# Split rows at byte 128 of 512, and one matmul of zeros in six gate blocks

## The chip, the cores and the metric

The kernel runs on one core of one Trainium2 chip. The metric is the device time of one execution in microseconds; the time of a kernel is the median of its runs. The engines are TensorE (PE, with its weight loads PEld), VectorE (DVE), ScalarE (ACT), GpSimd (POOL) and SyncE (SP), which issues the transfers of the weights.

## The reference

Two transformer blocks run one after the other on 256 tokens of width 1024, in float32. The first has two attentions, a gate and a feed-forward part; the second a gated delta rule with a sparse latent attention, a cross attention on 256 tokens of memory, and a feed-forward part of the same size. Cut to the parts that this text is about:

```python
# first block, D_FF = 2816
h = h + rms_norm(merged @ w_out, post_mix_gain)
u = rms_norm(h, pre_ffn_gain)
gate_up = u @ w_ffn_in                                   # 1024 -> 2 x 2816
f = (silu(gate_up[..., :D_FF]) * gate_up[..., D_FF:]) @ w_ffn_out
h = h + rms_norm(f, post_ffn_gain)
...
# second block
x = x + jnp.concatenate([o_dn, o_dsa], axis=-1) @ w_out
hx = rmsnorm(x, g_xattn)
qx = (hx @ w_xq).reshape(b, s, X_HEADS, X_DH)            # keys, values: mem @ w_xkv
...
x = x + ox @ w_xo
hf = rmsnorm(x, g_ffn)
x = x + (jax.nn.silu(hf @ w_gate) * (hf @ w_up)) @ w_down
return rmsnorm(x, g_final)
```

## The kernel before

Activations lie feature by feature: a tile of 1024 features by 256 tokens is 128 partitions by eight rows of 256 float32 numbers, 1024 bytes a row. A matmul on PE holds a 128 x 128 block of weights and streams one such row through it: the moving row.

A product is made of three matmuls in the format `float32r`: each operand is split into a high part (rounded) and a low part (the rest). For the weights `load_w` does it: a transfer on SP brings 512 KB into `raw`, ACT casts it to `wh` (L311), DVE subtracts to `wl` (L313); each has three buffers. For activations `split` does the same (`uh`, `ul`, and likewise `od`, `m`, `mem`, `mix`, `ox`, `f` with `_h` and `_l`). `gemm` makes one block of 128 output features: 24 matmuls, all at L326. Over the eight k they alternate `uh` x `wh` and `ul` x `wh`, sixteen in all, and then come eight of `uh` x `wl`; they add up in one bank of PSUM. A block is 24 matmuls whatever its activations are called.

`ffn_in` is a feed-forward stage's first half: for 22 values of j it makes a gate block (columns 2j of `w_gu`) and an up block (2j + 1), 44 blocks; DVE, ACT and POOL multiply, apply silu and split the result into `f_h`, `f_l`. `post_norm` ahead of the first stage and `residual` ahead of the second make `us`, the eight pairs of rows (uh, ul) that it reads, and return the norm's factors. `post_norm` and `residual` also run the blocks of `w_out1`, `w_fo1`, `w_out2` and `w_xo`; `gemm_long` is `gemm` over more than eight k. The blocks of `w_xq` (cross attention) read `us` of the same kind. `mem_keys` multiplies the memory's `mem_h`, `mem_l`, and it stands ahead of the first feed-forward stage.

Where a row starts in its partition follows from the tile's start and its row length. `new_u` makes tiles of [128, 8, 272] numbers of which 256 a row are used, so the rows lie 1088 bytes apart, which is 64 more than a multiple of 512. The first `u` of all is made in another way, as one long row of numbers from which eight rows of 256 are taken at number AT = 112:

```python
uh, ul = (gpool.tile([P, KT * NT + P], F32R, name="u" + e, tag="u" + e)[:, AT:AT + KT * NT].rearrange(
    "p (a b) -> p a b", a=KT) for e in "hl")
```

`sumsq` squares on ACT (`sq`, L403) and adds on DVE (L404). The order of each engine's instructions is chosen by a scheduler when the program is built, from the order of the code; a few lines are pinned. Tiles are placed, and buffers of a tag are added where memory is free, by the same step.

Of the kernel before, what the change touches and what calls it, by code (L numbers as in the profile page):

```python
# [16 lines left out]
F32 = mybir.dt.float32  # L17
F32R = mybir.dt.float32r
# [7 lines left out]
P = 128  # L26
NT = 256
NM = 16
NK = NT + NM
NP = NT + 32  # L30
D = 1024
KT = D // P
FF = 2816
FT = FF // P
# [175 lines left out]
GATES = [int(c) for c in "0010202020302022"]  # L210
BDLAST = 0
WARM = 12
AT = 112
RB = 2
MAGIC = float(0x5F3759DF)
SWAP = [i ^ 16 for i in range(32)]
# [4 lines left out]
def _program(tc, d, out):  # L221
    nc = tc.nc
    ctx = ExitStack()
    pe, act, dve, pool, sp = nc.tensor, nc.scalar, nc.vector, nc.gpsimd, nc.sync
# [7 lines left out]
    with ctx:  # L232
# [4 lines left out]
        gpool = new_pool(ctx, "gen")  # L237
# [75 lines left out]
            eng.tensor_tensor(l[:, :kt * c], raw[:, :kt * c], h[:, :kt * c].bitcast(F32), OP.subtract)  # L313
            return h, l

        def gemm(src, xs, n, use, first=True, last=True, ps=None, raw=None, late=()):

            kt = len(xs)
            h, l = load_w(src, kt, raw=raw)
            if ps is None:  # L320
                ps = mm.tile([P, 512], F32, name="mm", tag="mm")
            o = ps[:, :n]
            soon = [k for k in range(kt) if k not in late]
            steps = [(w, k, i) for ks in (soon, late) for w, i2 in ((h, 2), (l, 1)) for k in ks for i in range(i2)]
            for n_, (w, k, i) in enumerate(steps):
                pe.matmul(o, w[:, k * P:(k + 1) * P], xs[k][i], start=(first and n_ == 0),  # L326
                          stop=(last and n_ == len(steps) - 1))
            if last and use is not None:
                use(o)
            return ps  # L330
# [78 lines left out]
        def new_u():  # L409
            uh = gpool.tile([P, KT, NK], F32R, name="uh", tag="uh")  # L410
            ul = gpool.tile([P, KT, NK], F32R, name="ul", tag="ul")
            return uh, ul

# [5 lines left out]
        apool = new_pool(apx, "a")  # L422

        u = gpool.tile([P, KT, NK], F32, name="u", tag="u")
        uh, ul = (gpool.tile([P, KT * NT + P], F32R, name="u" + e, tag="u" + e)[:, AT:AT + KT * NT].rearrange(
            "p (a b) -> p a b", a=KT) for e in "hl")

        st = opool.tile([P, 512], F32, name="st", tag="o")
# [4 lines left out]
        for k in range(1, KT, 2):  # L433
            n = min(2, KT - k)
# [55 lines left out]
        at = ExitStack()  # L490
# [14 lines left out]
        def bank():  # L505

            began[0] += 1
            return ppool.tile([P, 512], F32, name="s", tag="s") if began[0] <= 3 else None
# [331 lines left out]
        rsm = mhp.tile([P, NT], F32, name="rsm")  # L840
        act.activation(rsm, st[:, :NT], AF.Copy)

        def post_norm(src_w, xs, gain, res, res_out, g_next, whole=False):

            fg = mpool.tile([P, 8, NT], F32, name="fg", tag="fg")
            acc = gpool.tile([P, NK], F32, name="acc", tag="acc", bufs=1)[:, :NT]
            for j in range(8):
                def use(o, j=j):
                    act.activation(fg[:, j, :], o, AF.Copy, scale=G(gain, j))
                    sumsq(j, o, acc, NT)  # L850
                gemm_long(src_w[j], xs, NT, use)
            rr = gpool.tile([P, NK], F32, name="rs", tag="rs", bufs=2)
            rsqrt_of(opool, acc, ones_d, NT, rr[:, :NT])
            if whole:
                u = gpool.tile([P, KT, NK], F32, name="u", tag="uh")
            else:
                uh, ul = new_u()
            acc2 = gpool.tile([P, NK], F32, name="acc2", tag="acc2", bufs=1)[:, :NT]
            for j in range(8):
                dve.tensor_tensor(fg[:, j, :], fg[:, j, :], rr[:, :NT], OP.mult)  # L860
                pool.tensor_tensor(res_out[:, j, :], fg[:, j, :], res[:, j, :NT], OP.add)
                if whole:
                    act.activation(u[:, j, :NT], res_out[:, j, :], AF.Copy, scale=G(g_next, j))
                else:
                    split(uh[:, j, :NT], ul[:, j, :NT], res_out[:, j, :], G(g_next, j))
                sumsq(j, res_out[:, j, :], acc2, NT)
            rs2 = gpool.tile([P, NK], F32, name="rs", tag="rs", bufs=2)
            rsqrt_of(opool, acc2, ones_d, NT, rs2[:, :NT])
            if whole:
                return [u[:, k, :NT] for k in range(8)], rs2[:, :NT]  # L870
            return [(uh[:, k, :NT], ul[:, k, :NT]) for k in range(8)], rs2[:, :NT]

        h1 = rpool.tile([P, KT, NT], F32, name="h1", tag="resB")
        us, rs = post_norm(d["w_out1"], [(m_h[:, k, :], m_l[:, k, :]) for k in range(8)],
                           "post_mix", hT, h1, "pre_ffn")

        def ffn_in(pool_, src_w, us, rs, f_h, f_l):
            for j in range(FT):
                sg = pool_.tile([P, NT], F32, name="sg", tag="sg", bufs=3)

                def use_g(o, sg=sg):
                    dve.tensor_tensor(sg, o, rs, OP.mult)  # L882
                    act.activation(sg, sg, AF.Silu)  # L883
                    pool.tensor_tensor(sg, sg, rs, OP.mult)  # L884

                def use_u(o, sg=sg, j=j):
                    t = pool_.tile([P, NT], F32, name="ft", tag="ft", bufs=2)
                    dve.tensor_tensor(t, o, sg, OP.mult)  # L888
                    split(f_h[:, j, :], f_l[:, j, :], t)

                bank = lambda i: ppool.tile([P, 512], F32, name="s", tag="s") if 2 * j + i < 3 else None
                gemm(src_w[2 * j], us, NT, use_g, ps=bank(0))
                gemm(src_w[2 * j + 1], us, NT, use_u, ps=bank(1))
            tc.keep_in_program_order(act.preload_act_table_set(EXP_LN))

# [64 lines left out]
        triu = CB("triu")  # L960
        ones_q = carve(P)
        dve.memset(ones_q, 1.0 / 256)
        mix_h = bpool.tile([P, 8, NT], F32R, name="mix_h")
        mix_l = bpool.tile([P, 8, NT], F32R, name="mix_l")

        sa = ExitStack()
        spool = new_pool(sa, "sa")
# [556 lines left out]

        added = []

        def residual(src_w, xs, res, res_out, g_next, late=(), more=0):
            uh, ul = new_u()
            acc = gpool.tile([P, NK], F32, name="acc", tag="acc", bufs=1)[:, :NT]
            for j in range(8):  # L1530
                def use(o, j=j):
# [7 lines left out]
            return [(uh[:, k, :NT], ul[:, k, :NT]) for k in range(8)], rs2[:, :NT]  # L1539

        x2 = rpool.tile([P, KT, NT], F32, name="x2", tag="resB")
        us, rs = residual(d["w_out2"], [(mix_h[:, k, :], mix_l[:, k, :]) for k in range(8)], x1, x2, "g_xattn", (0,1,2,3), 2)
        b2.close()


# [10 lines left out]
            return h, l  # L1556
        keys = [two("kx_", kx[:, 2 * h:2 * h + 2, :]) for h in range(4)]
        values = [two("vx_", vx[:, :, h * NT:(h + 1) * NT]) for h in range(4)]
        ox_h = xpool.tile([P, 8, NT], F32R, name="ox_h")
        ox_l = xpool.tile([P, 8, NT], F32R, name="ox_l")  # L1560
        rx = xpool.tile([P, 4], F32, name="rx")

        def query_scale():
# [41 lines left out]
                    pe.matmul(o[:, e, :], v_h, pt_l[:, mk, :], start=False, stop=(mk == 1))  # L1605
            split(ox_h[:, 2 * h:2 * h + 2, :], ox_l[:, 2 * h:2 * h + 2, :], o)
        x3 = rpool.tile([P, KT, NK], F32, name="x3", tag="resA")[:, :, :NT]
        us, rs = residual(d["w_xo"], [(ox_h[:, k, :], ox_l[:, k, :]) for k in range(8)], x2, x3, "g_ffn", (4,5,6,7), 2)
        xa.close()
        mst.close()  # L1610

# [7 lines left out]
        for qb in range(2):  # L1619
            for kk_ in range(2):  # L1620
# [1 line left out]
                for i in range(4):  # L1622
                    pe.transpose(t[:, i * P:(i + 1) * P], x3[:, 4 * kk_ + i, qb * P:(qb + 1) * P], ident)
                dve.tensor_copy(x3t[:, qb, kk_ * 512:(kk_ + 1) * 512], t)
        f_h = mpool.tile([P, FT, NT], F32R, name="f_h")
        f_l = mpool.tile([P, FT, NT], F32R, name="f_l")
        ffn_in(mpool, d["w_gu2"], us, rs, f_h, f_l)
        b1.close()
        accp = new_pool(fst, "ps_acc", 1, PSUM)
# [75 lines left out]
```

## Time and profile before

| | |
|---|---|
| time, median of 3 runs | 1013.58 us (1012.79 to 1014.91) |
| the profiled execution, its own time | 1014.82 us |
| its span | 1013.0 us |
| granted clock of PE, mean | 0.986 |
| busy: PE, PEld | 983.6 us (97%), 911.2 us (90%) |
| busy: DVE, ACT, POOL | 686.3 us (68%), 530.1 us (52%), 236.0 us (23%) |
| read from memory | 147.01 MB, 146 GB/s over the span |

Busy time counts an engine as busy while any of its instructions runs; matmuls overlap in the pipeline, so a busy PE says nothing of how closely they follow each other. That is read from the starts of matmuls in the timeline.

### The profile page before, as it was taken

To read this page: it belongs to the slowest core of one execution; us is meant where nothing else is said; L and a number is where in the kernel's file an instruction comes from. 1 tells how busy PE (TensorE), PEld (TensorE's weight loads), DVE (VectorE), ACT (ScalarE), POOL (GpSimd) and SP (SyncE) were. 2 spreads that over 40 slices of the span, in tenths; PEclk is the share of its full clock that TensorE was granted. 3 is DMA by queue.
4 is the path that set the end of the run, shared out by engine and by line. 5 is a ranking of instruction groups with operands and counts; after the bars stand their busy time and mean duration, and the time that the engine had idled before them with its cause. 6 is when DMAs were issued, how large, how long until landed. Compare 5 with 4: busy or idle time off the path is not lost.

```text
span 1013.0 us, 18580 instructions
## 1 busy us (share of the span) xinstructions
PE 983.6 (97%) x7196; PEld 911.2 (90%) x7196; DVE 686.3 (68%) x1478; ACT 530.1 (52%) x1077; POOL 236.0 (23%) x264
## 2 busy tenths in 40 slices
PE   9999999999969999999999899999999999999996
PEld 8878888988959999999999888788799999999885
DVE  5678678678796686656555638977787676666444
ACT  4456556556544556555554444335666555555433
POOL 5443325222290032121100302131021002212002
PEclk9999999999988999999999899999999999999998
DMA  5443332343443565555666232333046255555552
GB/s 199 140 152 105 110 119 84 110 140 105 148 138 132 191 197 181 183 187 186 200 216 199 94 127 91 123 115 109 1 148 207 66 186 187 188 187 189 182 192 84
DMA packets 42023, 149.26 MB, mean 147 GB/s; under 512 B 4728, under 2 KB 5376, under 8 KB 41808
## 3 DMA queue, kind: packets, MB, share of 16 engines
q1 hardware_dynamic: 40896, 145.47, 43.6%
q0 software_dynamic: 608, 2.03, 0.7%
q8 instruction: 56, 0.92, 0.4%
q10 hardware_dynamic: 432, 0.59, 0.2%
q14 instruction: 31, 0.25, 0.1%
HBM read 147.01 MB, written 1.06 MB: 146 GB/s over the span
## 4 chain that ended last, share of the span: by engine, by line
PE 86%; DVE 7%; POOL 3%; DMA 2%; ACT 1%; issue 1%; SPq 0%; ACTq 0%; DVEq 0%; POOLq 0%
PE mm L326 48%; PE mm L340 11%; PE s L524 3%; PE s L326 3%; PE ac L1639 2%; PE ac L1643 2%; PE ac L1642 2%; PE o L604 2%; DVE wl L313 1%; POOL memt L787 1%; DVE fg L860 1%; PE t L591 1%; POOL bd L767 1%; POOL memt L789 1%; PE mm L1401 1%; DMA memt<-memT 1%
## 5 line engine op out<-in xcount | busy, mean ns | idle before, releaser
L311 ACT ACTIVATE wh<-raw 128x1024 fp32r<-128x1024 f32 (+1 forms) x224 | 235.3, 1052 | 241.2 <-PE mm L326 147.6
L313 DVE TENSOR_TENSOR wl<-raw,wh 128x1024 fp32r<-128x1024 f32 (+1 forms) x230 | 282.6, 1230 | 108.3 <-ACT wh L311 104.4
L326 PE MATMUL mm<-uh,wh 128*128 128x256 f32 x968 | 239.0, 284 | 0.0
L326 PE MATMUL mm<-ul,wh 128*128 128x256 f32 x968 | 236.8, 282 | 0.0
L326 PEld LDWEIGHTS mm<-uh,wh 128*128 128x128 f32 x968 | 182.1, 188 | 2.7 <-ACT wh L311 0.6
L326 PEld LDWEIGHTS mm<-ul,wh 128*128 128x128 f32 x968 | 182.5, 189 | 0.7
L340 PE MATMUL mm<-u,raw 128*128 128x256 f32 (+1 forms) x608 | 145.5, 389 | 0.0
L326 PE MATMUL mm<-uh,wl 128*128 128x256 f32 x968 | 137.7, 282 | 0.0
L340 PEld LDWEIGHTS mm<-u,raw 128*128 128x128 f32 x608 | 111.7, 190 | 19.2 <-issue 1.0
L326 PEld LDWEIGHTS mm<-uh,wl 128*128 128x128 f32 x968 | 124.0, 189 | 0.2
L884 POOL TENSOR_TENSOR sg<-sg,rs 128x256 f32<-128x256 f32 x44 | 49.1, 1119 | 235.6 <-ACT sg L883 231.4
L888 DVE TENSOR_TENSOR ft<-mm,sg 128x256 f32<-128x256 f32 x42 | 17.8, 424 | 51.9 <-PE mm L326 51.4
L326 PE MATMUL mm<-f_h,wh 128*128 128x256 f32 x176 | 41.1, 276 | 0.0
L326 PE MATMUL mm<-f_l,wh 128*128 128x256 f32 x176 | 41.1, 276 | 0.0
L882 DVE TENSOR_TENSOR sg<-mm,rs 128x256 f32<-128x256 f32 x40 | 17.0, 424 | 32.2 <-PE mm L326 32.1
L1639 PE MATMUL ac<-wh,f_h 128*128 128x512 f32 (+1 forms) x110 | 38.4, 349 | 0.0
L1642 PE MATMUL ac<-wh,f_l 128*128 128x512 f32 (+1 forms) x110 | 38.1, 347 | 0.0
L1643 PE MATMUL ac<-wl,f_h 128*128 128x512 f32 (+1 forms) x110 | 37.8, 347 | 0.0
L326 PEld LDWEIGHTS mm<-f_l,wh 128*128 128x128 f32 x176 | 33.0, 188 | 0.0
L326 PEld LDWEIGHTS mm<-f_h,wh 128*128 128x128 f32 x176 | 33.0, 188 | 0.0
L499 POOL TENSOR_TENSOR ropem<-rawq,cqt 128x256 f32<-128x256 f32 x16 | 15.7, 979 | 49.5 <-ACT rawq L496 49.4
L287 ACT ACTIVATE f_h<-ft 128x256 fp32r<-128x256 f32 x44 | 18.3, 417 | 16.2 <-DVE ft L888 16.2
(546 smaller groups left out, 2134.3 us busy)
## 6 DMA issues: line engine op xcount, KB each, us to landing
raw<-w_gu SPq DMA_DIRECT2D x88, 512.0 KB, 4.1
raw<-w_dn SPq DMA_DIRECT2D x22, 512.0 KB, 3.5
raw<-w_pr SPq DMA_DIRECT2D x20, 512.0 KB, 3.5
raw<-w_gate SPq DMA_DIRECT2D x16, 512.0 KB, 3.4
raw<-w_out SPq DMA_DIRECT2D x16, 512.0 KB, 3.6
raw<-w_fo SPq DMA_DIRECT2D x16, 512.0 KB, 3.5
raw<-w_kb SPq DMA_DIRECT2D x8, 512.0 KB, 3.5
raw<-w_vb SPq DMA_DIRECT2D x8, 512.0 KB, 4.3
```

Of the source, the lines that this page charges most:

```text
L287: m = act.activation(h, src, AF.Copy)
L311: act.activation(h[:, :kt * c], raw[:, :kt * c], AF.Copy)
L313: eng.tensor_tensor(l[:, :kt * c], raw[:, :kt * c], h[:, :kt * c].bitcast(F32), OP.subtract)
L326: pe.matmul(o, w[:, k * P:(k + 1) * P], xs[k][i], start=(first and n_ == 0), stop=(last and n_ == len(steps) - 1))
L340: pe.matmul(o, raw[:, k * P:(k + 1) * P], x, start=(k == 0), stop=(k == len(xs) - 1))
L524: pe.matmul(os[c], a[half[c], tok], b[half[c]], start=(n == 0), stop=(last and n == 2))
L604: pe.matmul(o, a[kt], b[:, kt, :], start=(first and n == 0), stop=False)
L884: pool.tensor_tensor(sg, sg, rs, OP.mult)
L888: dve.tensor_tensor(t, o, sg, OP.mult)
L1639: m = pe.matmul(o, f_h[:, k, tok], h[:, cols], start=(k == 0), stop=False)
L1642: pe.matmul(o, f_l[:, k, tok], h[:, cols], start=False, stop=False)
L1643: pe.matmul(o, f_h[:, k, tok], l[:, cols], start=False, stop=(k == FT - 1))
```

## The change

The rows of the split activations get a start of their own. AT becomes a table by stage; `new_u_at` and `parts_at` make a tile as one long row with room to spare and take the eight rows of 1024 bytes from number `at` on. In the program that is built, the rows of `uh` and `ul` of both feed-forward stages, of the cross attention's `us`, of `mix` and of `ox` then start at byte 128 of 512; those of `f` and of the first `u` did so before, and those of `mem` stay as they were. Besides, in both feed-forward stages the gate blocks of j = 3, 6 and 12 take one more matmul behind their fourth: 96 rows of zeros as weights, the first 96 partitions of the same moving row, added to the same sum.

```diff
-AT = 112
+AT = {'ffn1': 112, 'xatt': 0, 'ffn2': 112, 'mem_h': 112, 'mem_l': 112, 'mix_h': 0, 'mix_l': 0, 'ox_h': 0, 'ox_l': 0, 'f': 0, 'first': 112}
...
-        def gemm(src, xs, n, use, first=True, last=True, ps=None, raw=None, late=()):
+        def gemm(src, xs, n, use, first=True, last=True, ps=None, raw=None, late=(), zero=None):
...
                 pe.matmul(o, w[:, k * P:(k + 1) * P], xs[k][i], start=(first and n_ == 0),
                           stop=(last and n_ == len(steps) - 1))
+                if zero is not None and n_ == 3:
+                    pe.matmul(o, zero, xs[k][i][:96], start=False, stop=False)
...
+        def rows_at(t, at):
+
+            return t[:, at:at + KT * NT].rearrange("p (a b) -> p a b", a=KT)
+
+        def new_u_at(at):
+            return [rows_at(gpool.tile([P, KT * NK], F32R, name="u" + e, tag="u" + e), at) for e in "hl"]
+
+        def parts_at(pool_, name, at_h, at_l):
+            return [rows_at(pool_.tile([P, KT * NT + P], F32R, name=name + e), at)
+                    for e, at in (("_h", at_h), ("_l", at_l))]
...
-                uh, ul = new_u()
+                uh, ul = new_u_at(at)
...
+            zeros = pool_.tile([96, P], F32R, name="zeros")
+            pool.memset(zeros.bitcast(F32), 0.0)
...
-                gemm(src_w[2 * j], us, NT, use_g, ps=bank(0))
+                gemm(src_w[2 * j], us, NT, use_g, ps=bank(0), zero=zeros if j in (3, 6, 12) else None)
...
-        mix_h = bpool.tile([P, 8, NT], F32R, name="mix_h")
-        mix_l = bpool.tile([P, 8, NT], F32R, name="mix_l")
+        mix_h, mix_l = parts_at(bpool, "mix", AT["mix_h"], AT["mix_l"])
...
-        def residual(src_w, xs, res, res_out, g_next, late=(), more=0):
-            uh, ul = new_u()
+        def residual(src_w, xs, res, res_out, g_next, late=(), more=0, at=0):
+            uh, ul = new_u_at(at)
...
-        ox_h = xpool.tile([P, 8, NT], F32R, name="ox_h")
-        ox_l = xpool.tile([P, 8, NT], F32R, name="ox_l")
+        ox_h, ox_l = parts_at(xpool, "ox", AT["ox_h"], AT["ox_l"])
...
-        f_h = mpool.tile([P, FT, NT], F32R, name="f_h")
-        f_l = mpool.tile([P, FT, NT], F32R, name="f_l")
+        f_h, f_l = (mpool.tile([P, FT * NT + P], F32R, name=n)[:, AT["f"]:AT["f"] + FT * NT].rearrange(
+            "p (a b) -> p a b", a=FT) for n in ("f_h", "f_l"))
```

On PE, at the gate block of j = 3 in the first feed-forward stage, this is the order before; `mm` is the bank of PSUM, and the first row is the end of the up block of j = 2.

```order
L326 MATMUL mm<-uh,wl 128x256 x8
L326 MATMUL mm<-uh,wh 128x256
L326 MATMUL mm<-ul,wh 128x256
L326 MATMUL mm<-uh,wh 128x256
L326 MATMUL mm<-ul,wh 128x256
L326 MATMUL mm<-uh,wh 128x256
L326 MATMUL mm<-ul,wh 128x256
```

In the changed program the same place reads:

```order
L328 MATMUL mm<-uh,wl 128x256 x8
L328 MATMUL mm<-uh,wh 128x256
L328 MATMUL mm<-ul,wh 128x256
L328 MATMUL mm<-uh,wh 128x256
L328 MATMUL mm<-ul,wh 128x256
L331 MATMUL mm<-ul,zeros 128x256
L328 MATMUL mm<-uh,wh 128x256
L328 MATMUL mm<-ul,wh 128x256
```

The matmul of zeros stands between the second and the third k; nothing else has moved on PE.

On ACT, in the norm that ends the first block (`x` is the residual, `u` the next rows), this is the order before, with the engines whose semaphores an instruction waits for in brackets.

```order
L863 ACTIVATE u<-x_6203,base 128x256 [waits Pool_49]
L400 ACTIVATE acc_6928<-x_6203 128x256
L863 ACTIVATE u<-x_6203,base 128x256 [waits Pool_49]
L403 ACTIVATE sq<-x_6203 128x256
L863 ACTIVATE u<-x_6203,base 128x256 [waits Pool_49]
L403 ACTIVATE sq<-x_6203 128x256
L863 ACTIVATE u<-x_6203,base 128x256 [waits Pool_49] x2
L403 ACTIVATE sq<-x_6203 128x256
```

In the changed program:

```order
L878 ACTIVATE u<-x_6208,base 128x256 [waits Pool_49]
L404 ACTIVATE acc_6933<-x_6208 128x256
L878 ACTIVATE u<-x_6208,base 128x256 [waits Pool_49]
L407 ACTIVATE sq<-x_6208 128x256 [waits DVE_49]
L878 ACTIVATE u<-x_6208,base 128x256 [waits Pool_49]
L407 ACTIVATE sq<-x_6208 128x256
L878 ACTIVATE u<-x_6208,base 128x256 [waits Pool_49] x2
L407 ACTIVATE sq<-x_6208 128x256 [waits DVE_49]
```

The instructions stand in the same order; `sq` has fewer buffers, and some of its squares wait for DVE's sums.

On POOL, at the start of the program, the two memsets stand ahead of the first squares (`s`, of the input `hT`):

```order
L715 MEMSET va_h 128x1024
L716 MEMSET va_l 128x1024
L717 MEMSET vam 96x512
L894 MEMSET zeros 96x128 x2
L461 ISA
L461 TENSOR_TENSOR s_128<-hT 128x272
```

Both were absent before; the rest of POOL's order is unchanged.

## Rows read from the trace of the kernel before

**Rows 1.** The page, part 4: the chain that ended last, share of the span by line.

```profile
PE mm L326 48%; PE mm L340 11%; PE s L524 3%; PE s L326 3%; PE ac L1639 2%; PE ac L1643 2%; PE ac L1642 2%; PE o L604 2%; DVE wl L313 1%; POOL memt L787 1%; DVE fg L860 1%; PE t L591 1%; POOL bd L767 1%; POOL memt L789 1%; PE mm L1401 1%; DMA memt<-memT 1%
```

**Rows 2.** Waits, 390 to 490 us: who for whom, us, times, longest.

```profile
ACT wh L311 <- PE mm L326: 35.2, 35, 1.1
```

**Rows 3.** Windows: from:to, length, each engine's busy time (instructions), PEclk, DMA share, GB/s.

```profile
269.40:279.40 10.00, 10.00 (x90) 10.00 (x89) 7.40 (x17) 3.44 (x7) 3.03 (x2) 1.00 0.54 206
348.40:362.00 13.60, 13.60 (x115) 13.60 (x115) 13.30 (x20) 9.33 (x18) 8.32 (x9) 1.00 0.34 111
395.00:490.00 95.00, 95.00 (x805) 95.00 (x804) 57.16 (x84) 49.83 (x67) 19.44 (x17) 1.00 0.57 184
500.00:550.00 50.00, 50.00 (x443) 50.00 (x443) 24.81 (x27) 24.43 (x35) 0.30 (x1) 1.00 0.69 214
564.00:580.00 16.00, 12.14 (x80) 11.85 (x79) 13.04 (x23) 7.58 (x17) 7.94 (x8) 0.79 0.24 82
```

**Rows 4.** Timeline of PE, first feed-forward stage: start, us, instruction.

```profile
440.48 1.10 PE L326 MATMUL mm<-uh,wl 128*128 128x256 f32 x8
...
446.16 1.10 PE L326 MATMUL mm<-uh,wl 128*128 128x256 f32 x8
```

**Rows 5.** Timeline of PE, the memory's keys.

```profile
353.03 1.12 PE L326 MATMUL mm<-mem_h,wl 128*128 128x256 f32 x8
```

**Rows 6.** Timeline of PE, the branch of `od`.

```profile
272.83 1.07 PE L326 MATMUL mm<-od_h,wl 128*128 128x256 f32 x8
...
278.27 1.07 PE L326 MATMUL mm<-od_h,wl 128*128 128x256 f32 x8
```

**Rows 7.** Timeline of PE, first projections: the first stretch, and the block at 74.59.

```profile
19.05 1.07 PE L326 MATMUL s<-uh,wl 128*128 128x256 f32 x8
...
74.59 0.36 PE L326 MATMUL mm<-uh,wh 128*128 128x256 f32 x1
74.79 0.28 PE L326 MATMUL mm<-ul,wh 128*128 128x256 f32 x1
...
76.56 1.10 PE L326 MATMUL mm<-uh,wl 128*128 128x256 f32 x8
```

**Rows 8.** Timeline of PE: stretches behind a matmul of 96 rows (L606), first and last.

```profile
196.98 0.28 PE L606 MATMUL o<-pm,vam 96*128 96x256 f32 x1
...
198.25 0.73 PE L326 MATMUL mm<-uh,wl 128*128 128x256 f32 x5
...
269.06 0.28 PE L606 MATMUL o<-pm,vam 96*128 96x256 f32 x1
...
270.11 1.07 PE L326 MATMUL mm<-od_h,wl 128*128 128x256 f32 x8
```

**Rows 9.** Timeline of PE: blocks of `w_out2`, `w_xq` and `w_xo`.

```profile
745.93 1.08 PE L326 MATMUL mm<-mix_h,wl 128*128 128x256 f32 x8
748.72 1.08 PE L326 MATMUL mm<-mix_h,wl 128*128 128x256 f32 x8
...
767.84 1.10 PE L326 MATMUL mm<-uh,wl 128*128 128x256 f32 x8
...
810.04 1.13 PE L326 MATMUL mm<-ox_h,wl 128*128 128x256 f32 x8
```

**Rows 10.** Timeline of POOL, the start; in brackets idle time before, and its releaser.

```profile
3.05 0.51 POOL L702 MEMSET vam<- 96x512 f32 x1
5.11 1.30 POOL L446 TENSOR_TENSOR s<-hT 128x272 f32<-128x272 f32 x2 [1.55 <-DMA hT<-hT]
```

**Rows 11.** Timeline of ACT, DVE and PE in the norm that ends the first block.

```profile
571.30 0.40 ACT L403 ACTIVATE sq<-x 128x256 f32<-128x256 f32 x1
...
574.30 0.51 ACT L863 ACTIVATE u<-x,base 128x256 f32<-128x256 f32 x1
...
573.12 1.96 DVE L404 TENSOR_TENSOR acc<-acc,sq 128x256 f32<-128x256 f32 x3
...
579.18 3.62 PE L340 MATMUL mm<-u,raw 128*128 128x256 f32 x16
```

**Rows 12.** Timeline of PE in the stage of `w_bs`, at the low clock.

```profile
309.27 1.91 PE L326 MATMUL mm<-os_h,wl 128*128 128x256 f32 x8
```

More of the change, by code (lines that the diff above doesn't have):

```diff
@@ L424, in _program @@
         u = gpool.tile([P, KT, NK], F32, name="u", tag="u")
-        uh, ul = (gpool.tile([P, KT * NT + P], F32R, name="u" + e, tag="u" + e)[:, AT:AT + KT * NT].rearrange(
+        uh, ul = (gpool.tile([P, KT * NT + P], F32R, name="u" + e, tag="u" + e)[:, AT["first"]:AT["first"] + KT * NT].rearrange(
             "p (a b) -> p a b", a=KT) for e in "hl")
@@ L841, in _program, with post_norm @@
         act.activation(rsm, st[:, :NT], AF.Copy)
-        def post_norm(src_w, xs, gain, res, res_out, g_next, whole=False):
+        def post_norm(src_w, xs, gain, res, res_out, g_next, at=0, whole=False):
             fg = mpool.tile([P, 8, NT], F32, name="fg", tag="fg")
@@ L874, in _program @@
         us, rs = post_norm(d["w_out1"], [(m_h[:, k, :], m_l[:, k, :]) for k in range(8)],
-                           "post_mix", hT, h1, "pre_ffn")
+                           "post_mix", hT, h1, "pre_ffn", at=AT["ffn1"])
         def ffn_in(pool_, src_w, us, rs, f_h, f_l):
+            zeros = pool_.tile([96, P], F32R, name="zeros")
+            pool.memset(zeros.bitcast(F32), 0.0)
             for j in range(FT):
@@ L1541, in _program @@
         x2 = rpool.tile([P, KT, NT], F32, name="x2", tag="resB")
-        us, rs = residual(d["w_out2"], [(mix_h[:, k, :], mix_l[:, k, :]) for k in range(8)], x1, x2, "g_xattn", (0,1,2,3), 2)
+        us, rs = residual(d["w_out2"], [(mix_h[:, k, :], mix_l[:, k, :]) for k in range(8)], x1, x2, "g_xattn", (0,1,2,3), 2, AT["xatt"])
         b2.close()
@@ L1607, in _program @@
         x3 = rpool.tile([P, KT, NK], F32, name="x3", tag="resA")[:, :, :NT]
-        us, rs = residual(d["w_xo"], [(ox_h[:, k, :], ox_l[:, k, :]) for k in range(8)], x2, x3, "g_ffn", (4,5,6,7), 2)
+        us, rs = residual(d["w_xo"], [(ox_h[:, k, :], ox_l[:, k, :]) for k in range(8)], x2, x3, "g_ffn", (4,5,6,7), 2, AT["ffn2"])
         xa.close()
```

## Prediction

> **What bounds the kernel now.** I began with the page: the chain that ended last spends 48% of the span at one line, L326, the matmul of `gemm`; no other line has more than 11% [rows 1]. So what a matmul of that line costs, from its start to the next start, is the first thing to know. Second, the waits of a stretch deep in the first feed-forward stage: the cast of the weights waits for PE, 35.2 us in 35 waits of 100 us [rows 2]. The buffers are full and PE is what the others wait for, so a shorter beat on PE shortens the stage.
>
> Third, the granted clock: it is 1.00 in the stretches that I compare [rows 3]. Fourth, the beat, from the timeline. The eight `wl` matmuls of a block show as one row, which lasts seven beats and the last matmul. In the feed-forward stage two blocks lie 5.68 us apart, so 2.84 us a block or 118.3 ns for each of its 24 matmuls [rows 4]. The same instruction with weights of the same shape goes at other beats elsewhere: in the memory's keys (1.12 - 0.28) / 7 = 120 ns [rows 5], in the `od` branch 5.44 us for two blocks, 113.3 ns [rows 6]. What differs is where the moving rows start. In the built program every block of `wh` and `wl` starts at byte 192 of 512. The rows of `mem_h` and `mem_l` start at 192 too: 120 ns. Those of `od`, `m` and `f` start at 128: 113.3 ns. The feed-forward rows are 1088 bytes apart and so start at 192, 256, ... 448, 0, 64, 128 in turn: 118.3 ns, between the two.
>
> Byte 128 alone does not settle it. The `u` rows of the first projections start there as well. From 15 to 300 us I find 44 stretches of nine or more matmuls over rows at 128: 32 go at 113 to 114 ns after their first five, 12 stay near 117.7 ns to their end. The first stretch and the last hold the short beat; one with the long beat is the block at 74.59 [rows 7, 8]. So there are two steady beats, and what stood ahead of a stretch decides into which it falls. Behind a matmul of 96 rows (L606) four of these stretches begin, and all four take the short beat; the first and the last of the four are shown [rows 8].
>
> **The change part by part.** The order on every engine is as before but for six matmuls and two memsets, so I count beats.
>
> *Feed-forward stages.* There are 44 blocks a stage, 88 in all. From 2.84 to 2.72 us saves 0.12 us a block: 10.56 us. The first blocks lie beside DVE's normalization and partly at the low clock, where a matmul takes 0.21 us whatever its row's byte, so I take off 0.25: **-10.3**. In the long beat a block takes 24 x 117.7 = 2.82 us, and all 88 save 1.4 us.
>
> *Queries of the cross attention* (`w_xq`). They read the same kind of `u`: eight blocks at the mixed beat now, (1.10 - 0.28) / 7 = 117 ns [rows 9]. They are cut up by scores and transposes, and each cut chooses the beat anew: between 0 and 8 x 0.12 = 0.96; I take **-0.6**.
>
> *`w_out2`.* `mix_l` moves from 192 to 128. A block takes 2.79 us now [rows 9], 2.72 in the short beat, so -0.5 for eight; in the long beat +0.3. I take **-0.4**.
>
> *`w_xo`.* `ox` moves from 192 to 128, from (1.13 - 0.28) / 7 = 121 ns, the steady 120 with one longer step [rows 9], to 113.3: 8 x 0.16 = 1.28, or 0.45 in the long beat. Taken: **-1.0**.
>
> *Six matmuls of zeros.* A matmul of 96 rows lasts 0.28 us, as one of 128 does [rows 8], so it takes one beat, 0.12 us, and the four or five behind it some 5 ns more each until the beat is steady: 6 x 0.15 = **+0.9**. If each also cost the 0.20 us that a stretch's first matmul takes behind a transpose [rows 7] in place of a beat, it would be 1.4.
>
> *Memsets of the zeros.* Both stand on POOL directly ahead of the first squares, where POOL idles 1.55 us for the first transfer; a memset four times as wide takes 0.51 us [rows 10]. Two small ones fit: 0. Without that idle time they would cost about 0.3.
>
> *Waits that moved with the tiles.* The tiles lie elsewhere, and some get fewer buffers. In the norm that ends the first block, ACT's `sq` now waits for a sum of DVE. The `sq` at 571.30 would wait for DVE's first sum, which starts at 573.12, some 2 us; the last `u`, at 574.30, slides by about as much. PE comes to the projections that read `u` only at 579.18, behind the memory's values [rows 11]. Hidden: 0. Without the values in front it would be up to 3 us.
>
> *Tiles that nobody meant to move.* The `os` rows of `w_bs` stay a mixture of bytes, and part of that stage runs at the low clock: 0, within 0.7 either way (four blocks' worth at full clock, 0.16 each). Keys and queries of the first attention move too: 96 pairs of score matmuls at the 7 ns between the two beats, again within 0.7 either way, taken as 0.
>
> Sum: -10.3 - 0.6 - 0.4 - 1.0 + 0.9 = **-11.4 us**. The profiled execution took 1014.82 us (span 1013.0, 1.8 around it), which gives 1003.4. It lies 1.2 above the median of the three runs, 1013.58, and medians are compared: **1002.2 us**.
>
> *A rule that speaks against it.* By the rows, the byte at which a row starts moves the beat from 113 to 120 ns [rows 5, 6]. The Trainium skill, TensorE: Matmul & The Clock Gate, section Step-by-step: what each phase is for, has it that PE reads the moving operand and the next weights through two independent ports, so that loading weights takes no read bandwidth from the running matmul. By that rule only the zeros would be left, 6 x 0.12 = +0.7 us. The trace disagrees; it has its rival below.
>
> **The rivals.** *The long beat.* A feed-forward stage, or most of it, locks at 117.7 ns. For it: 12 of 44 stretches. Against: the four behind 96 rows, and three such matmuls a stage. Not known: whether one can also throw the short beat into the long one; the last leaves some 20 blocks with nothing behind it. A whole stage costs 44 x 0.10 = 4.4 us: 1006.6; 20 blocks 2 us: 1004; both stages 1011.
>
> *Nothing comes of it.* The byte only goes together with something else in the stages that I compared, and the zeros cost their beats: 1013.6 + 0.7 = 1014.3, within 0.2%. Against: 120, 118.3 and 113.3 ns stand with equal shapes at one clock.
>
> *Weights come late and the clock falls* (slower). A block would now want 512 KB every 2.72 us, 193 GB/s, where the stage moves 184 [rows 3]. If PE ran dry between blocks, its granted clock could fall to 1.2 GHz, where it stands for part of 564 to 580 (0.79 over the stretch [rows 3]), after PE had waited for DVE. A matmul then takes (1.91 - 0.41) / 7 = 214 ns [rows 12], a block 5.1 us, 2.4 more than in the short beat. Five such blocks eat the 11.4 us; from the sixth on the kernel is slower, 1016.6; ten make 1026. Against: the weights' cast waits 1.0 us a block for PE, eight times the 0.12 by which the block shrinks [rows 2], and 214 GB/s flow in the stage behind [rows 3].
>
> **How the numbers follow.** Short beat in both stages, 1000.5 to 1003.5: 0.70. Long in one stage or a good part of one, 1003.5 to 1008: 0.14. Long in both, about 1011: 0.06. Nothing: 0.06. Late weights: 0.04. The low clock between 564 and 580 covers (1 - 0.79) x 16 / 0.5 = 6.7 us, at most 3.4 us of delay, and could come out shorter or longer in a program whose stages have moved: 1.7 either way. With every term at its best (-12.7) and that, 999.2 is the low end; the high end, 1008, takes in one stage at the long beat and leaves out 0.16 above it. 0.2% (2 us) is about what a measurement of this kernel can tell from no change. Long in both lies at that edge and is counted half as faster, half as same: faster 0.87, same 0.09, slower 0.04.
>
> **What would show it.** Blocks of both feed-forward stages 2.72 us apart and rows of eight `wl` at 1.07 us, against 1.10 where the beat is long; a change of beat, if any, at the blocks with zeros; `w_xo` at 1.07. The cast of the weights should still wait for PE, and the granted clock should stay 1.00 from 395 us to the end of the stage. It is wrong if blocks stay near 2.82 us behind the last zeros, if PE waits for `wl` inside the stages, or if the clock falls there.

## Result, and the profile after

The changed kernel takes 1002.43 us (median of 5 runs, 1001.82 to 1005.1), the kernel before 1013.58 beside it (5 runs): ratio 0.9893, 95% interval 0.988 to 0.9907, so 11.15 us less. The prediction was 1002.2. The profiled execution took 1002.38 us, its span 1000.6 against 1013.0, 12.4 less.

The chain by line [rows 1], and the waits from 384 to 484 us, 6 us earlier than those of [rows 2]:

```profile
PE mm L328 48%; PE mm L344 12%; PE s L539 3%; PE s L328 2%; PE ac L1658 2%; PE ac L1657 2%; PE ac L1654 2%; PE o L619 2%; DVE wl L314 1%; POOL memt L802 1%; DVE fg L875 1%; PE t L606 1%; POOL bd L782 1%; POOL memt L804 1%; PE mm L1417 1%
```

```profile
ACT wh L312 <- PE mm L328: 33.4, 35, 1.2
```

The windows that answer to two of [rows 3], and one that holds the end of the memory's keys (columns as there); behind them, by itself, that last window in the kernel before:

```profile
389.00:484.00 95.00, 95.00 (x840) 95.00 (x839) 59.99 (x87) 51.59 (x70) 21.31 (x18) 1.00 0.60 194
558.00:574.00 16.00, 12.12 (x83) 11.75 (x82) 12.93 (x23) 7.47 (x17) 7.96 (x8) 0.89 0.24 81
362.00:390.00 28.00, 26.77 (x219) 25.35 (x218) 24.38 (x48) 16.41 (x26) 4.84 (x9) 1.00 0.71 233
```

```profile
362.00:390.00 28.00, 26.76 (x201) 25.32 (x200) 22.89 (x46) 14.49 (x24) 4.36 (x8) 0.94 0.68 222
```

`gemm` still ends last; the cast still waits for PE; the stage moves 194 GB/s where 193 was worked out, at the granted clock 1.00. Two stretches have a higher clock than before: 558 to 574 stands at 0.89 ([rows 3]: 0.79), and 362 to 390 at 1.00, where the kernel before had 0.94. Neither goes with the change: the kernel with zeros alone (below), which gained nothing, spent as little time at the low clock in both places as the changed one, and the kernel with zeros of 128 rows, which gained as much, stood at 0.94 from 360 to 390.

The timeline of PE, first stage (behind the matmul of `cc`, and at the zeros of j = 12), second stage (its first whole blocks and first zeros), `w_out2` and `w_xo`:

```profile
381.90 0.81 PE L939 MATMUL s<-cc,base 32*8 32x384 f32 x2
384.64 1.10 PE L328 MATMUL mm<-uh,wl 128*128 128x256 f32 x8
386.05 0.28 PE L331 MATMUL mm<-ul,zeros 96*128 96x256 f32 x1
387.54 1.07 PE L328 MATMUL mm<-uh,wl 128*128 128x256 f32 x8
...
431.19 1.07 PE L328 MATMUL mm<-uh,wl 128*128 128x256 f32 x8
433.91 1.07 PE L328 MATMUL mm<-uh,wl 128*128 128x256 f32 x8
435.27 0.28 PE L331 MATMUL mm<-ul,zeros 96*128 96x256 f32 x1
436.77 1.07 PE L328 MATMUL mm<-uh,wl 128*128 128x256 f32 x8
...
748.20 1.07 PE L328 MATMUL mm<-mix_h,wl 128*128 128x256 f32 x8
...
809.96 1.11 PE L328 MATMUL mm<-ox_h,wl 128*128 128x256 f32 x8
...
824.80 1.11 PE L328 MATMUL mm<-uh,wl 128*128 128x256 f32 x8
827.62 1.11 PE L328 MATMUL mm<-uh,wl 128*128 128x256 f32 x8
829.04 0.28 PE L331 MATMUL mm<-ul,zeros 96*128 96x256 f32 x1
830.54 1.07 PE L328 MATMUL mm<-uh,wl 128*128 128x256 f32 x8
```

The first stage behind `cc` and the second from its start were in the long beat (2.82 us from 824.80 to 827.62) until the first matmul of zeros, and in the short one (2.72, from 431.19 to 433.91) from there to the end; the later zeros do not disturb it and cost 0.14 each (436.77 - 433.91 = 2.86). The last block of `w_xo` falls into the long beat (809.96), between first matmuls of the second stage, which is long from there on.

The same matmul on PE, before and after, gives the account of the 12.4 us:

| up to this matmul (its start before) | after minus before | what lies in between |
|---|---|---|
| 8.28 | +0.47 | the first transfer lands later |
| 360.11 | +0.10 | |
| 372.06 | -1.48 | no time at the low clock ahead of the first stage |
| 498.11 | -6.04 | first feed-forward stage, -4.56 |
| 560.11 | -6.04 | `w_fo1`, rows at 128 as before |
| 588.03 | -6.67 | the low clock is shorter: (1 - 0.79) x 16 / 0.5 = 6.7 us, now (1 - 0.89) x 16 / 0.5 = 3.5 |
| 660.05 | -5.52 | PE waits for DVE (at 646.68 after) |
| 756.02 | -6.12 | `w_out2`, -0.47 of it |
| 757.20 | -5.55 | the norm behind it takes that back |
| 788.19 | -6.15 | queries, -0.60 |
| 819.03 | -7.12 | `w_xo`, -0.97 |
| 944.22 | -11.38 | second feed-forward stage, -4.26 |
| 1003.01 | -12.16 | `w_down`, -0.78 |

### The profile page after: what moved, and what is told of

It is laid out like the page before. It is cut to its first block, busy times and chain, and to the rows that moved or that the text cites. A ratio compares the mean times of both kernels' runs of the same rounds, so it can differ in the third digit from the quotient of the medians.

```text
span 1000.6 us, 18596 instructions
## 1 busy us (share of the span) xinstructions
PE 969.4 (97%) x7202; PEld 896.8 (90%) x7202; DVE 685.7 (69%) x1478; ACT 524.6 (52%) x1077; POOL 237.5 (24%) x266
## 4 chain that ended last, share of the span: by engine, by line
PE 86%; DVE 8%; POOL 3%; ACT 1%; issue 1%; DMA 0%; SPq 0%; ACTq 0%; DVEq 0%
PE mm L328 48%; PE mm L344 12%; PE s L539 3%; PE s L328 2%; PE ac L1658 2%; PE ac L1657 2%; PE ac L1654 2%; PE o L619 2%; DVE wl L314 1%; POOL memt L802 1%; DVE fg L875 1%; PE t L606 1%; POOL bd L782 1%; POOL memt L804 1%; PE mm L1417 1%
## 5 line engine op out<-in xcount | busy, mean ns | idle before, releaser
L328 PE MATMUL mm<-uh,wh 128*128 128x256 f32 x968 | 233.1, 281 | 0.0
L328 PE MATMUL mm<-ul,wh 128*128 128x256 f32 x968 | 230.8, 279 | 0.3 <-DVE ul L292 0.3
L344 PE MATMUL mm<-u,raw 128*128 128x256 f32 (+1 forms) x608 | 145.5, 389 | 0.0
L328 PE MATMUL mm<-uh,wl 128*128 128x256 f32 x968 | 134.7, 279 | 0.0
L344 PEld LDWEIGHTS mm<-u,raw 128*128 128x128 f32 x608 | 111.7, 190 | 19.3 <-issue 1.0
L328 PEld LDWEIGHTS mm<-uh,wl 128*128 128x128 f32 x968 | 121.1, 188 | 0.2
L900 ACT ACTIVATE sg<-sg 128x256 f32<-128x256 f32 x44 | 18.1, 418 | 31.2 <-DVE sg L899 31.1
```

The lines of the kernel that those rows point to most:

```text
L344: pe.matmul(o, raw[:, k * P:(k + 1) * P], x, start=(k == 0), stop=(k == len(xs) - 1))
```

## The experiments

Theory: rows at 128 have two steady beats, and a matmul of zeros brings the short one. Rivals: the beat finds back to the short one by itself and the zeros only cost; the zeros do it all and the byte nothing.

**The byte without the zeros, and the zeros without the byte.** In the first, `ffn_in` loses its zeros:

```diff
-            zeros = pool_.tile([96, P], F32R, name="zeros")
-            pool.memset(zeros.bitcast(F32), 0.0)
...
-                gemm(src_w[2 * j], us, NT, use_g, ps=bank(0), zero=zeros if j in (3, 6, 12) else None)
+                gemm(src_w[2 * j], us, NT, use_g, ps=bank(0), zero=None)
```

> The changed kernel without the six matmuls of zeros and without their memsets; all rows stay at byte 128. Theory A (two steady beats, and a matmul of 96 rows sets the short one): the second feed-forward stage, which in the changed kernel began with three blocks 2.826 us apart, stays at that distance to its end (41 more blocks by 0.106 = +4.3 us), and w_down behind it takes 2.78 us a k as before the change instead of 2.74 (+0.8); the first stage stays long behind the matmul of `cc` at 382 us (about 40 blocks, +4.2); the six matmuls save 0.85. Sum: 1002.4 + 8.5 = 1010.9 us, 1006 if only one stage stays long. Theory B (the beat finds back to the short one by itself, the zeros only cost): 1001.6 us, blocks 2.72 us apart in both stages.

The second is the kernel before with these lines and the extra matmul of `gemm` added:

> The kernel before with the six matmuls of zeros and their memsets alone; rows stay at their mixture of bytes. Theory A (the byte makes the beat, the zeros only choose between two beats that rows at 128 have): blocks stay 2.84 us apart, six of them 2.98: 1013.6 + 0.85 = 1014.4 us. Rival (the zeros did it all, the bytes nothing): blocks fall to 2.72 us behind the first zeros of each stage, about 40 of 44 in each, 80 x 0.12 - 0.85 = -8.8: 1004.8 us.

Without the zeros: 1013.23 us (11 runs, 1011.43 to 1016.84), ratio to the kernel before 0.9995 (0.9982 to 1.0007): the gain is gone. Zeros alone: 1014.53, ratio 1.0007 (0.9997 to 1.0016). Neither half moves the time by itself; together they give 11.15 us. The timeline of the kernel without zeros, at the end of the first stage and in `w_fo1`, and at the end of the second stage:

```profile
492.17 1.10 PE L328 MATMUL mm<-uh,wl 128*128 128x256 f32 x8
495.00 1.10 PE L328 MATMUL mm<-f_h,wl 128*128 128x256 f32 x8
...
940.24 1.11 PE L328 MATMUL mm<-uh,wl 128*128 128x256 f32 x8
```

Both stages are long to their last block, as the theory had it, and the long beat is handed on into `w_fo1`, whose eight `f_h` x `wl` took 1.07 before and in the changed kernel: 528 matmuls x 4.4 ns = 2.3 us, which the expectation lacked. `w_down`, which it had long (+0.8), was short from its third k on. So 1010.9 + 2.3 - 0.8 = 1012.4, beside 1013.23 measured where the kernel before took 1013.8. The byte alone does do something: by the same comparison of matmuls as in the table, `w_xo` is 0.96 us shorter and `w_down` 0.71 without any zeros, and the long `w_fo1` takes 2.25 back. With zeros alone the blocks stay 2.84 us apart, behind the zeros too (timeline):

```profile
437.18 0.28 PE L329 MATMUL mm<-ul,zeros 96*128 96x256 f32 x1
...
441.54 1.10 PE L326 MATMUL mm<-uh,wl 128*128 128x256 f32 x8
444.38 1.10 PE L326 MATMUL mm<-uh,wl 128*128 128x256 f32 x8
```

**Zeros with 128 rows, and zeros in j = 0.**

```diff
-            zeros = pool_.tile([96, P], F32R, name="zeros")
+            zeros = pool_.tile([P, P], F32R, name="zeros")
...
-                    pe.matmul(o, zero, xs[k][i][:96], start=False, stop=False)
+                    pe.matmul(o, zero, xs[k][i], start=False, stop=False)
```

> The changed kernel, but each of the six matmuls of zeros has 128 rows instead of 96. Theory A1 (what sets the short beat is the change of the number of rows): a matmul of 128 rows does nothing, so the second stage stays at 2.826 us a block, +4.3, w_down +0.8, and the first stage perhaps too, +4.2: 1007.5 to 1011.7 us. Theory A2 (any matmul that stands outside the pairs of uh and ul does it): as the changed kernel, 1002.4 us, blocks 2.72 us apart from the first zeros on.

```diff
-                gemm(src_w[2 * j], us, NT, use_g, ps=bank(0), zero=zeros if j in (3, 6, 12) else None)
+                gemm(src_w[2 * j], us, NT, use_g, ps=bank(0), zero=zeros if j == 0 else None)
```

> The changed kernel with one matmul of zeros a stage, in the first gate block (j = 0), instead of three. Theory A (what last broke the stream sets the beat): the second stage is short from its first block on (3 blocks by 0.106 = -0.3) and has two zeros less (-0.3); in the first stage the zeros now stand ahead of the matmul of `cc`, which at 382 us began a block with the long beat, so the stage stays long to its end: about 40 blocks, +4.2, less 0.3. Sum: 1002.4 + 3.3 = 1005.7 us. Rival (the long block behind `cc` is a chance of that run, or the beat comes back by itself): both stages short, 1002.4 - 0.9 = 1001.5 us.

128 rows: 1003.28 us (1002.24 to 1004.11), ratio 0.9889 (0.9875 to 0.9902). The 96 rows are not what counts. Zeros in j = 0 alone: 1008.0 us (1006.62 to 1010.95), ratio 0.994 (0.9926 to 0.9955); the timelines of the two, the second at `cc` and in the second stage:

```profile
829.03 1.11 PE L328 MATMUL mm<-uh,wl 128*128 128x256 f32 x8
830.45 0.28 PE L331 MATMUL mm<-ul,zeros 128*128 128x256 f32 x1
831.93 1.07 PE L328 MATMUL mm<-uh,wl 128*128 128x256 f32 x8
```

```profile
381.29 1.07 PE L328 MATMUL mm<-uh,wl 128*128 128x256 f32 x8
382.29 0.81 PE L939 MATMUL s<-cc,base 32*8 32x384 f32 x2
385.03 1.10 PE L328 MATMUL mm<-uh,wl 128*128 128x256 f32 x8
...
828.27 1.07 PE L328 MATMUL mm<-uh,wl 128*128 128x256 f32 x8
```

The matmul of `cc` throws the first stage from the short beat into the long one, and zeros that stand ahead of it are lost; that stage and `w_fo1` (+2.3 again, which is the miss of the expectation) stay long. The second stage is short from its first block on.

**Zeros in every gate block, behind matmul j of block j.**

```diff
-                if zero is not None and n_ == 3:
+                if zero is not None and n_ == zat:
...
-                gemm(src_w[2 * j], us, NT, use_g, ps=bank(0), zero=zeros if j in (3, 6, 12) else None)
+                gemm(src_w[2 * j], us, NT, use_g, ps=bank(0), zero=zeros, zat=j)
```

> The changed kernel with a matmul of zeros in all 22 gate blocks of both stages, in block j behind matmul number j (the first is 0), so that it stands behind uh and behind ul, and among the wh and among the wl. Theory A (whatever breaks the stream brings the short beat): all blocks short from the first zeros behind `cc` on; 38 more zeros by 0.14 = +5.3, and the second stage's first three blocks short, -0.3: 1007.4 us. Theory B (the place in the block decides which beat follows): about half of them, or a third, are followed by the long beat until the next zeros; with 15 of 44 long, 30 blocks by 0.106 = +3.2 more: 1010.6 us, and the list of places shows which.

1006.91 us (1006.61 to 1010.03), ratio 0.9939 (0.9919 to 0.9958). Of the 44 matmuls of zeros 41 stand in an unbroken stream: all 41 are followed by the short beat, 40 of them out of the short beat and one (behind `cc`) out of the long one. The place in the block does not matter, and in these blocks a matmul of zeros never brought the long beat.

**Rows at eight bytes, with weights at 192 and at 0.** `rows_of` takes the rows of block b from number (112 + 16 (b // 5)) mod 128 of the same tiles:

```diff
-                gemm(src_w[2 * j], us, NT, use_g, ps=bank(0), zero=zeros if j in (3, 6, 12) else None)
-                gemm(src_w[2 * j + 1], us, NT, use_u, ps=bank(1))
+                    gemm(src_w[b], rows_of(whole, b), NT, use, ps=bank(i), zero=zeros if b % 5 == 2 else None)
```

> The changed kernel, but the 44 blocks of the second feed-forward stage read their rows at other places of the same two tiles, five blocks at each byte: 128, 192, 256, 320, 384, 448, 0, 64 of 512, then four with uh at 128 and ul at 192; of every five the third has a matmul of zeros. The stage's numbers are not the reference's (rows are shifted). Weights stay at 192. Theory (the byte alone makes the beat, and eight bytes in turn give the mean that the kernel before had): 113.3 ns at 128, 120.0 at 192, and the other six on the average (8 x 118.3 - 113.3 - 120.0) / 6 = 118.9 ns; two beats at 128 alone. Rival (a row must not begin at the byte of the weights, all others are alike): 120 at 192 and one beat near 114 to 118 at the other seven. The time is not what is asked; by the theory about 1002.4 + 35 x 24 x 0.0055 = 1007 us.

The other kernel has besides:

```diff
-            h = wpool.tile([P, KT * P], F32R, name="wh", tag="wh" + tag, bufs=3)
-            l = wpool.tile([P, KT * P], F32R, name="wl", tag="wl" + tag, bufs=3)
+            h, l = (wpool.tile([P, KT * P + 128], F32R, name="w" + e, tag="w" + e + tag, bufs=3)[:, 80:80 + KT * P]
+                    for e in "hl")
```

> As the kernel with eight bytes, and wh and wl start at byte 0 of 512 instead of 192 in the whole kernel. Theory R (what counts is the row's byte less the weights' byte): the series is that of the other kernel moved by 192, so the short beat of rows at 128 goes to rows at 448 (128 - 192 + 512), the 120 ns of rows at 192 goes to rows at 0, and the first feed-forward stage, with rows at 128, has the beat that the other kernel shows at 320. Theory M (the row's byte alone counts): 113.3 ns still at 128, 120 still at 192, the first stage at 2.72 us a block as in the changed kernel.

The timeline of the first of them: a block ahead of the zeros and one behind them at 192, and a block each at 320, 384 and 0:

```profile
833.28 1.12 PE L328 MATMUL mm<-uh,wl 128*128 128x256 f32 x8
836.28 1.12 PE L328 MATMUL mm<-uh,wl 128*128 128x256 f32 x8
...
864.96 1.11 PE L328 MATMUL mm<-uh,wl 128*128 128x256 f32 x8
...
876.17 1.07 PE L328 MATMUL mm<-uh,wl 128*128 128x256 f32 x8
...
904.60 1.10 PE L328 MATMUL mm<-uh,wl 128*128 128x256 f32 x8
```

And of the second, weights at 0: two blocks of the first stage, rows at 128, and of the second stage the groups at 192, 256 and 448:

```profile
409.96 1.11 PE L328 MATMUL mm<-uh,wl 128*128 128x256 f32 x8
412.81 1.11 PE L328 MATMUL mm<-uh,wl 128*128 128x256 f32 x8
...
846.58 1.11 PE L328 MATMUL mm<-uh,wl 128*128 128x256 f32 x8
848.00 0.28 PE L331 MATMUL mm<-ul,zeros 96*128 96x256 f32 x1
849.49 1.07 PE L328 MATMUL mm<-uh,wl 128*128 128x256 f32 x8
...
863.62 1.12 PE L328 MATMUL mm<-uh,wl 128*128 128x256 f32 x8
...
906.38 1.07 PE L328 MATMUL mm<-uh,wl 128*128 128x256 f32 x8
```

The distances of whole blocks without zeros, over 24, sort by the row's byte less the weights' byte, modulo 256:

| row minus weights, mod 256 | rows, weights at 192 | rows, weights at 0 | us a block | ns a matmul |
|---|---|---|---|---|
| 0 | 192, 448 | 0, 256 | 2.880 | 120.0 |
| 64 | 0, 256 | 64, 320 | 2.827 | 117.8 |
| 128 | 64, 320 | 128, 384 | 2.844 to 2.852 | 118.5 to 118.8 |
| 192 | 128, 384 | 192, 448 | 2.720, or 2.827 ahead of zeros | 113.3 or 117.8 |

Theory R holds, and with a period of 256 bytes, not 512: the first stage, rows still at 128, went to 2.845 to 2.852 us a block when only the weights moved (at one piece of it, between the zeros of j = 3 and j = 6, to 2.88, so there are two beats at this difference as well, and there the zeros of j = 3 brought the longer one). In these blocks the zeros brought the short beat only at 192; at two of the four groups there (384 with weights at 192, 448 with weights at 0) the stream was short ahead of the zeros already. Neither expectation of the first kernel came out whole: 120 ns stands at 448 too, and the short beat at 384 too. The two kernels took 1009.95 and 1024.36 us, one execution each.

**The rows of the other stages.** `mix_h`, `mix_l`, `ox_h`, `ox_l` and the rows of `w_xq` are made as before the change:

```diff
-            uh, ul = new_u_at(at)
+            uh, ul = new_u() if at is None else new_u_at(at)
...
-        us, rs = residual(d["w_out2"], [(mix_h[:, k, :], mix_l[:, k, :]) for k in range(8)], x1, x2, "g_xattn", (0,1,2,3), 2, AT["xatt"])
+        us, rs = residual(d["w_out2"], [(mix_h[:, k, :], mix_l[:, k, :]) for k in range(8)], x1, x2, "g_xattn", (0,1,2,3), 2, None)
```

> The changed kernel with mix, ox and the rows of w_xq as before the change; only the rows of the two feed-forward stages stand at 128, with the six matmuls of zeros. By the terms of the prediction the three other edits gave 0.4 + 0.6 + 1.0 = 2.0 us: 1004.4. By the trace of the changed kernel w_out2 and w_xo gave 0.4 and 1.0, w_xq nearly nothing: 1003.8. Rival (the three give nothing that lasts to the end): 1002.4.

> The changed kernel once more, on the chip and beside the runs of the two others: 1002.4 us, with the second stage's first three blocks and the block behind cc at the long beat if what chooses the beat there is fixed by the program, and with other blocks if it is chance.

The first takes 1003.53 us (1002.86 to 1005.51), the changed kernel again 1002.13 (1001.48 to 1004.69); ratios to the kernel before beside them 0.9893 (0.9877 to 0.991) and 0.9882 (0.9864 to 0.9899). The medians are 1.4 us apart, where the terms said 2.0; the intervals overlap, so the sum of the three is not shown by times, only stage by stage in the table above. Nor are the two alike in the rest: the trace of the first has no wait of PE for DVE at that place, which costs 1.15 us in the table. In the trace of that second run of the changed kernel the same blocks are long: the one behind `cc`, and the second stage up to its first zeros.

**A version that goes further.** One matmul of zeros a stage (j = 3, and j = 0 in the second), and the memory's rows at 128:

```diff
-        mem_h = mhp.tile([P, 8, NT], F32R, name="mem_h")
-        mem_l = mhp.tile([P, 8, NT], F32R, name="mem_l")
+        mem_hl = mhp.tile([P, 2 * KT * NT], F32R, name="mem_hl").rearrange(
+            "p (a b) -> p a b", b=NT)
+        mem_h, mem_l = mem_hl[:, :8, :], mem_hl[:, 8:, :]
```

> The changed kernel with one matmul of zeros a stage, where the runs so far say that it does its work (j = 3 in the first stage, behind `cc`; j = 0 in the second), and with mem_h and mem_l in one tile whose rows start at byte 128 instead of 192; the weights stay at 192. Theory A: four zeros less -0.56, the first three blocks of the second stage short -0.3; the memory's keys 8 blocks by 24 x 6.7 ns = -1.3; its values, 192 matmuls of which mem is the weights' side, -0.9 if that side counts too, part of them at 1.2 GHz or not on the path. Sum: 1002.4 - 3.0 = 999.4 us. If the mem stages fall into the long beat instead, 2.3 ns a matmul remain: 1000.7. Rival (the byte does nothing where mem is concerned, DVE sets that stage): 1001.5 us.

And with four zeros more, two in the memory's values and two in `w_xo` (blocks 2 and 4; this cut shows the first two):

```diff
+                            if kk_ == 1 and tb == 0 and g in (0, MEMG):
+                                pe.matmul(o, zeros, h[:96, cols], start=False, stop=False)
```

> The kernel with one matmul of zeros a stage and mem at 128, and four more matmuls of zeros: two in the memory's values, which ran at 117.7 ns there (192 matmuls, 144 in one piece, by 4.4 ns: -0.6 to -0.8, less 0.3), and two in w_xo (blocks 2 and 4 of 8, the third of which fell into the long beat in the changed kernel: up to 6 blocks by 0.1, less 0.3). Theory (a matmul of zeros brings the short beat wherever the row stands 64 bytes ahead of the weights): values at 113.3 ns behind the first zeros also where it is mem that is the weights' side; 0.4 to 0.7 us less than the kernel without these four, against the changed kernel -1.5 to -2.5: about 1000.4 us where the changed kernel has 1002.4. Rival (in these short stages each cut chooses the beat anew, so the kicks are lost): +0.5.

They take 1001.99 us (1000.04 to 1002.86), ratio 0.9878 (0.9857 to 0.9899), and 1003.86 (1002.62 to 1007.98), ratio 0.9901 (0.988 to 0.9921): neither can be told from the changed kernel, and both miss what was expected (999.4 and 1000.4). The first moves its keys to the short beat, as expected (timeline):

```profile
347.47 1.07 PE L328 MATMUL mm<-mem_hl,wl 128*128 128x256 f32 x8
```

against 1.12 [rows 5], but its profiled execution stood at 1.2 GHz for 3.4 us at 366.5, where that of the changed kernel did not. The values of the two kernels, where the second has its zeros (timelines, the first kernel, then the second):

```profile
550.57 0.28 PE L825 MATMUL mm<-wh,mem_hl 128*128 128x256 f32 x1
...
554.30 0.28 PE L825 MATMUL mm<-wh,mem_hl 128*128 128x256 f32 x1
```

```profile
551.08 0.28 PE L830 MATMUL mm<-wh,zeros 96*128 96x256 f32 x1
...
551.31 0.28 PE L827 MATMUL mm<-wh,mem_hl 128*128 128x256 f32 x1
...
554.85 0.28 PE L827 MATMUL mm<-wh,mem_hl 128*128 128x256 f32 x1
```

The first goes at 113 ns (33 matmuls in 3.73 us) and falls to 117.7 only behind a small float32 matmul at 554.65. The second starts at 113 as well and goes at 118 from the zeros on (30 matmuls in 3.54 us). So here one matmul of zeros threw the short beat into the long one, and the theory falls. In these matmuls `wh` streams from 192 and mem is the weights, at 128: the difference is 64. The blocks of the table had one beat there; here, and in `w_down` (below), whose difference is 64 too, there are both. In `w_xo` the zeros of one block turned the long beat into the short one (117.9 to 113.2 ns at 798.82); those of the other stand in a stream that is cut again at once. `w_xo` as a whole came out no shorter with the two (0.59 us less than in the kernel before, against 0.57 without them and 0.97 in the changed kernel).

**What makes the long beat.** Behind `cc` the long beat came, out of the short one, in the changed kernel and in all ten other traces with those rows at 128 and the weights at 192. A small float32 matmul like it was put into the second stage:

```diff
+                if us2 and j in (8, 16):
+                    s = ppool.tile([P, 512], F32, name="s", tag="s")
+                    tc.keep_in_program_order(
+                        pe.matmul(s[:8, :NT], zeros[:32, :8].bitcast(F32), us[0][0][:32].bitcast(F32),
+                                  start=True, stop=True))
```

> The changed kernel, and in the second feed-forward stage a small float32 matmul of zeros (32 rows of 8 weights, its result unused) stands ahead of the gate blocks of j = 8 and j = 16, as the float32 matmul of `cc` stands in the first stage; the zeros of j = 3, 6 and 12 stay. Theory (a float32 matmul between blocks throws the stream into the long beat, as behind cc in every kernel so far): blocks 2.72 us apart from j = 3 to 7, 2.826 from j = 8 to 11, 2.72 from the zeros of j = 12 on, 2.826 from j = 16 to the end; 8 + 11 blocks by 0.106 = +2.0 and two cuts of some 0.7 us: about 1005.9 us. Rival (cc is followed by the long beat for another reason, such as what stands there besides): blocks stay 2.72 us apart all along, +1.4 for the cuts: 1003.8 us.

It took 1003.23 us; the timeline at j = 8:

```profile
854.52 1.07 PE L328 MATMUL mm<-uh,wl 128*128 128x256 f32 x8
855.52 0.59 PE L912 MATMUL s<-uh,zeros 32*8 32x256 f32 x2
...
857.99 1.07 PE L328 MATMUL mm<-uh,wl 128*128 128x256 f32 x8
```

The theory falls: in these blocks a float32 matmul as such does not bring the long beat (at j = 16 neither). What `cc` has besides (384 columns, another tile) was not tried, nor whether a pause or a matmul of something else than zeros would bring the short beat.

## Why the prediction was right, and where it was not

*Feed-forward stages, -10.3, and zeros, +0.9.* The sum of the two, -9.4, was measured as -4.56 - 4.26 = -8.8; the rest is the blocks ahead of the first zeros, four or so in the second stage and one or two in the first, 0.1 us each. A matmul of zeros cost 0.13 to 0.15, as taken. But the sum books the 10.3 under the byte and the zeros as a cost; that zeros bring the short beat stands only in the argument against the long one. The runs show that neither half earns the 10.3: the byte alone gives nothing that can be measured in the whole (ratio 0.9995), because both stages then lock at the long beat. "Long in both" had 0.06 of the chance for the kernel as it is; for the same kernel without zeros it is what happens, and `w_fo1` then goes long with them. The reason given for the short beat (four stretches behind 96 rows, all short [rows 8]) was the right observation; the 96 rows in it were not the cause, 128 do the same.

*Not known: whether zeros can throw the short beat into the long one.* In the blocks that the prediction speaks of, no: 0 of 40. In the memory's values, one did.

*`w_xq` -0.6, `w_out2` -0.4, `w_xo` -1.0.* Measured -0.60, -0.47, -0.97; 0.57 of it is given back where PE waits for the norm behind `w_out2`, which the prediction did not have. So `w_out2` gained nothing in the end: from its first matmul to the one behind that wait, the changed kernel takes 0.04 us longer.

*Not in the sum: `w_down`, -0.78.* Its bytes are the same before and after. Its 256-wide matmuls went at 117.9 ns before and 113.4 after, so there are two beats here as well. That the stage ahead hands its beat on is not shown: without zeros the second stage ends long, and `w_down` is short from its third k on. The timelines of before and of after, rows three matmuls apart (0.36 and 0.34 us by their starts, rounded):

```profile
954.16 0.28 PE L1639 MATMUL ac<-wh,f_h 128*128 128x256 f32 x1
...
954.52 0.28 PE L1639 MATMUL ac<-wh,f_h 128*128 128x256 f32 x1
```

```profile
942.66 0.28 PE L1654 MATMUL ac<-wh,f_h 128*128 128x256 f32 x1
...
943.00 0.28 PE L1654 MATMUL ac<-wh,f_h 128*128 128x256 f32 x1
```

*Memsets, moved waits: 0.* The memsets (0.34 us at 3.52) lie in POOL's idle time, and `sq` waits for DVE as worked out, 2.31 us, while PE comes to these rows only at 572.51 (timelines of ACT and PE):

```profile
567.69 0.42 ACT L407 ACTIVATE sq<-x 128x256 f32<-128x256 f32 x1 [2.31 <-DVE acc L408]
...
572.51 3.62 PE L344 MATMUL mm<-u,raw 128*128 128x256 f32 x16
```

*The clock.* In the profiled executions 2.2 us of the 12.4 come from two stretches at the low clock that were shorter or absent; the prediction allowed 1.7 for one of them. The kernel with zeros alone shows the same 2.2 without any gain (1014.53 us), so they tell nothing of the change. PE's wait for DVE at 646.68, which both traces of the changed kernel have, takes 1.15 back; the prediction did not have it.

*The total.* The median moved by 11.15. The beats alone add up to 4.56 + 4.26 + 0.60 + 0.47 + 0.97 + 0.78 = 11.64, less the 0.57 behind `w_out2` 11.07, but the wait for DVE and the later first transfer (0.47) stand against them in the same trace, and the clock with them; how these divide in the medians was not measured. That -11.4 came so near is in part luck: `w_down`, which was not in the sum, made up for the 0.6 missing in the feed-forward stages. The best case of the prediction adds up to -12.6 by its own terms, not -12.7, so its low end is 0.1 too low.

*The rule.* Moving the weights alone changed the beat of untouched rows, from 2.72 to about 2.85 us a block. Where a row and the weights lie therefore matters together. By the Trainium skill (TensorE: Matmul & The Clock Gate, section Step-by-step: what each phase is for) the two are read through two independent ports, and loading weights takes no read bandwidth from the running matmul. The traces disagree in so far as the beat hangs on both starts; by what part of the chip it does, no run shows.

## What to carry to other kernels

When the same matmul goes at different beats in different stages, look at the byte of its moving row less that of its weights, and look at whole stages, not at one stretch: in both feed-forward stages a beat, once taken, held to the end, and from the first into `w_fo1`. Where two beats are possible, one matmul of zeros for 0.14 us was worth 4.5 us a stage (second stage, one at j = 0: 5.13 us less than before, against 0.65 with none), and its place is behind whatever throws the stream off. Where the difference is another, try it first: in the memory's values it brought the long beat. Test both halves of such a change alone before giving either the credit.

## What the runs showed of the hardware that was not expected

Blocks of 24 matmuls of 256 columns repeat at 113.3, 117.8, 118.5 to 118.8 or 120.0 ns a matmul, by the difference of two start bytes modulo 256, at one granted clock of 1.00. At a difference of 192 there are two beats with nothing else changed, and 40 blocks stayed in the long one without finding back; at 64 there are both in `w_down` and in the memory's values. Float32 matmuls (L344) show nothing of the kind, though their rows start at all eight bytes in turn: 16 in 3.62 us. What chooses the beat at the start of a stage, and why `cc` brought the long one in 11 of 11 traces, stays open.
